# A recurrence in chunks: transition, input and output matrices formed ahead of the chain

## The chip, the cores and the metric

The kernel runs on one core of a Trainium2 chip. The metric is the device time of one execution in microseconds. Three runs of the kernel before took 3712.27, 3714.47 and 3717.64 us; the median is 3714.47 us. A change of 0.2%, about 7 us, is near what such runs can tell apart.

## What is computed

A two-layer encoder trunk over 1024 tokens of width 1024, in fp32: layer 0 mixes tokens by attention, layer 1 by a recurrence of the RWKV-7 kind in both directions, and each layer has an MLP. The change is in the recurrence of layer 1. Each of 16 heads holds a 64 x 64 state in each direction:

```python
def rwkv7_scan(r, w, k, v, kk, a):
    def step(state, inp):
        r_t, w_t, k_t, v_t, kk_t, a_t = inp
        sa = jnp.einsum('bhvk,bhk->bhv', state, -kk_t)
        state = (state * w_t[:, :, None, :] + sa[..., None] * (kk_t * a_t)[:, :, None, :]
                 + v_t[..., None] * k_t[:, :, None, :])
        return state, jnp.einsum('bhvk,bhk->bhv', state, r_t)
```

Direction 1 runs over the tokens backwards. The outputs are group-normed, gated and summed over the directions after this.

## The kernel before

The whole recurrence is in `rwkv_scan`. Tokens are cut into chunks of 64. Within a chunk the recurrence is written in closed form: with the decays divided out, the coupling between the tokens of a chunk is a strictly triangular 64 x 64 matrix per head, its unit-triangular inverse is applied to the chunk's inputs, and the state is carried from chunk to chunk.

The work goes by groups. A group is two chunks (128 tokens) of four heads (two pairs of heads) in both directions, so it has four chains (pair x direction, two heads in each) of two chunks each. Four groups are a batch, two batches are all tokens of four heads, and there are 32 groups. For each group:

- `prep` loads the group's decays, keys and receptances, makes exponentials, forms `zr` and `bk`, and multiplies them into `af` (L1266), which holds the coupling matrices in 64 columns and the in-chunk output matrices in the next 64. It masks `af` on POOL (L1270), transposes `bk` into `bn` (L1278, L1280) and writes the couplings to memory (`nd`, L1284). It runs eight groups ahead, in nine slots of buffers.
- `invert`, once a batch, reads the four diagonal 32 x 32 blocks of all couplings back, inverts them on DVE by 30 steps of two operations (L1297, L1299), writes them out, and puts them into `af` by DMAs (L1315, L1317).
- `post` makes the centered values (L1338 into `sv`) and completes the inverse's off-diagonal block by two products of 32 x 32 tiles (L1352, L1363).
- `scan` is the chain. For each chunk and each of the four chains: `c` <- coupling x values + `zr` x state (L1388, L1392); a copy of it to `y`, one half on ACT, the other on DVE (L1394, L1395); `c` <- inverse x `y` (L1397); copies into the other half of `sv` (L1399, L1400); `c` <- `bn` x `sv` (L1403); the new state `h` by two operations on DVE with the decay `pc` and the decayed old state `hd` that ACT made (L1386, L1412); and the output from `sv` and the old state (L1418, L1423), copied to `ot` (L1426). The operands of two heads stand in one 128-row matrix with zeros in the other head's place, so each product has 128 rows, and two heads write the two column halves of the array.
- `finish` does the group norm (L1445 is its one product), the gate and the sum, and stores.

The functions that do the side work are generators. After each chain's step of `scan`, `side` moves each of three lists of them on by a step. The order in which instructions then stand in the queues is set by a scheduler at build time, which goes by priorities (the chain's is raised) and its own times; at run time every engine works its queue in that order, and SP issues all these DMAs from one queue.

## Time and profile before

| | |
|---|---|
| profiled execution | 3712.8 us |
| its span on the core | 3710.7 us |
| granted TensorE clock over the span | 0.904 |
| PE, DVE, ACT, POOL busy over the span | 3197.8, 2596.9, 1854.2, 1850.4 us |
| L1266, first and last start (preparation) | 1937.9, 2756.2 us |
| first L1388 (chain) and last L1426 | 2122.2, 2909.2 us |

The span is one execution on the core. An engine's busy time is the time in which at least one of its instructions runs; matmuls are pipelined, so a busy PE need not be PE at its peak. PEld is the loading of weights, which overlaps PE. The recurrence with its preparation lies between about 1940 and 2915 us; attention and the first MLP are ahead of it, the output projection and the second MLP behind. A row of a view that groups instructions has: line, engine, operation, output<-inputs, shapes, count | busy us, mean ns of one | idle time of the engine just before, and what ended it.

### The profile page before, as it was taken

Reading aid. Unit: us, or ns where it says so; the run is one execution under the profiler, and the core shown is the slowest. Engines: PE = TensorE matmul, PEld = TensorE weight load, DVE = VectorE, ACT = ScalarE, POOL = GpSimd, SP = SyncE. Lnnn points to the kernel's source line nnn. Section 1 sums busy time; section 2 is a strip of 40 time slices with the busy share of each in tenths; the row PEclk is TensorE's granted clock in tenths of the full one; section 3 lists DMA queues with packets and bytes.
Section 4 is the critical chain, followed back from the end, with each engine's and each line's share of the span. In section 5 each row is a group of like instructions: output and inputs, shape, how many; then the busy total and the mean of one; then the engine's idle time right before and its main releaser. Section 6 shows DMA issues by size and latency. Waiting matters only on the chain. (4 is left out here: it accounts for less than half of the span.)

```text
span 3710.7 us, 61321 instructions
## 1 busy us (share of the span) xinstructions
PE 3197.8 (86%) x22168; PEld 2599.8 (70%) x22168; DVE 2596.9 (70%) x4617; ACT 1854.2 (50%) x4244; POOL 1850.4 (50%) x1642
## 2 busy tenths in 40 slices
PE   7999989799998978878888687787787889999998
PEld 6788987688777755555566575666666667887776
DVE  3355564744599979986963678888886565449996
ACT  2366564455543345654533365556566445554333
POOL 1000001655598877754566434444331146558887
PEclk9999999899999989879987587788787899999999
DMA  6222224232322032248766444444443413223023
GB/s 199 71 78 88 70 74 153 92 118 103 108 91 114 12 127 74 82 143 230 230 209 189 112 111 112 111 122 120 119 109 114 137 65 148 106 80 142 28 87 114
DMA packets 425100, 425.70 MB, mean 115 GB/s; under 512 B 138667, under 2 KB 338475, under 8 KB 418652
## 3 DMA queue, kind: packets, MB, share of 16 engines
q1 hardware_dynamic: 423612, 417.58, 36.3%
q0 software_dynamic: 1184, 4.20, 0.4%
q8 instruction: 174, 2.85, 0.3%
q14 instruction: 130, 1.06, 0.1%
HBM read 290.83 MB, written 138.20 MB: 116 GB/s over the span
## 5 line engine op out<-in xcount | busy, mean ns | idle before, releaser
L101 PE MATMUL pm<-bhi,lo 128*128 128x512 f32 x840 | 333.1, 399 | 46.3 <-DVE lo L130 46.1
L130 DVE TENSOR_TENSOR lo<-x,hi 128x512 fp32r<-128x512 f32 x300 | 322.1, 1080 | 61.8 <-ACT hi L129 61.7
L129 ACT ACTIVATE hi<-x 128x512 fp32r<-128x512 f32 x300 | 189.6, 633 | 323.4 <-DVE x L127 126.5
L100 PE MATMUL pm<-blo,hi 128*128 128x512 f32 x840 | 331.8, 395 | 8.6 <-POOL blo L130 8.1
L99 PE MATMUL pm<-bhi,hi 128*128 128x512 f32 x840 | 320.5, 394 | 5.4 <-ACT bhi L129 5.0
L127 POOL TENSOR_TENSOR x<-w1r 128x512 f32<-128x512 f32 x160 | 214.0, 1341 | 202.1 <-DVE lo L130 178.1
L130 POOL TENSOR_TENSOR blo<-bx,bhi 128x512 fp32r<-128x512 f32 x138 | 222.3, 1612 | 26.6 <-ACT bhi L129 26.0
L1270 POOL TENSOR_TENSOR af<-af,amask 128x512 f32<-128x512 f32 x128 | 163.8, 1286 | 136.7 <-ACT af L1269 111.9
L101 PEld LDWEIGHTS pm<-bhi,lo 128*128 128x128 f32 x840 | 158.4, 189 | 99.1 <-DVE lo L130 67.6
L905 POOL TENSOR_TENSOR wl<-wr,wh 128x512 fp32r<-128x512 f32 (+2 forms) x144 | 188.8, 1322 | 77.1 <-ACT wh L904 57.1
L1266 PE MATMUL A<-zr,bk 128*128 128x128 f32 x1024 | 187.4, 346 | 44.3 <-DVE bk L1259 38.1
L127 POOL TENSOR_TENSOR bx<-w 128x512 f32<-128x512 f32 x140 | 215.5, 1541 | 9.5
L886 DVE SCALAR_TENSOR_TENSOR x<-u,mu,x 128x512 f32<-128x512 f32 x192 | 208.4, 1121 | 7.9 <-ACT x L884 5.7
L1266 PEld LDWEIGHTS A<-zr,bk 128*128 128x128 f32 x1024 | 166.5, 249 | 58.6 <-POOL bk L1260 21.0
L127 DVE TENSOR_TENSOR x<-h 128x512 f32<-128x512 f32 x140 | 195.5, 1408 | 5.3 <-ACT h L268 2.7
L100 PEld LDWEIGHTS pm<-blo,hi 128*128 128x128 f32 x840 | 159.0, 189 | 49.5 <-POOL blo L130 16.0
L99 PEld LDWEIGHTS pm<-bhi,hi 128*128 128x128 f32 x840 | 159.3, 190 | 38.9 <-ACT bhi L129 5.9
L99 PE MATMUL mm<-xmh,wh 128*128 128x512 f32 x384 | 168.5, 460 | 17.0 <-ACT xmh L890 6.5
L1418 PE MATMUL c<-af,sv 128*64 128x64 f32 x1024 | 97.5, 275 | 79.8 <-DVE h L1412 71.2
L100 PE MATMUL mm<-xml,wh 128*128 128x512 f32 x384 | 157.1, 412 | 7.6 <-DVE xml L891 7.6
L1412 DVE SCALAR_TENSOR_TENSOR h<-c,pc,hd 64x64 f32<-64x64 f32 x448 | 126.8, 283 | 47.9 <-PE c L1403 30.3
L583 ACT ACTIVATE S<-S,mneg 128x256 f32<-128x256 f32 (+2 forms) x256 | 125.2, 501 | 67.0 <-DVE mneg L578 44.1
(370 smaller groups left out, 10044.3 us busy)
## 6 DMA issues: line engine op xcount, KB each, us to landing
w1r<-in_mlp_w_dram SPq DMA_DIRECT2D x32, 1024.0 KB, 5.4
w<-in_mlp_w_dram SPq DMA_DIRECT2D x32, 1024.0 KB, 5.5
x<-x SPq DMA_DIRECT2D x64, 386.0 KB, 3.4
hd<-h SPq DMA_DIRECT2D x24, 1024.0 KB, 4.2
h<-hd SPq DMA_DIRECT2D x24, 1024.0 KB, 7.8
wr<-in_w_rkv_dram SPq DMA_DIRECT2D x96, 256.0 KB, 2.8
rk<-rk SPq DMA_DIRECT2D x64, 256.0 KB, 3.9
x<-cs SPq DMA_DIRECT2D x32, 260.0 KB, 3.9
```

What stands on the lines that cost most here:

```text
L99: nc.tensor.matmul(out, lhsT=ahi, rhs=bhi, start=start, stop=False)
L100: nc.tensor.matmul(out, lhsT=ahi, rhs=blo, start=False, stop=False)
L101: nc.tensor.matmul(out, lhsT=alo, rhs=bhi, start=False, stop=stop)
L127: add.tensor_tensor(out=y, in0=x, in1=blocks[term[2]], op=ALU.add if term[1] == "+" else ALU.subtract)
L129: nc.scalar.activation(hi, x, AF.Copy)
L130: sub.tensor_tensor(out=lo, in0=x, in1=hi, op=ALU.subtract)
L583: nc.scalar.activation(s[:, :n], s[:, :n], AF.Exp, bias=mneg[:, i:i + 1], scale=-1.0)
L886: nc.vector.scalar_tensor_tensor(out=x, in0=at(2 * i), scalar=mu[:, i, c, kt:kt + 1], in1=x, op0=ALU.mult, op1=ALU.add)
L905: nc.gpsimd.tensor_tensor(out=wlo, in0=wr, in1=whi, op=ALU.subtract)
L1266: nc.tensor.matmul(ps[:, fsl(u, P)], lhsT=bk[:, u, j].rearrange("p a b -> p (a b)"), rhs=zr[:, u].rearrange("p a b -> p (a b)"), start=Tru ...
L1270: nc.gpsimd.tensor_tensor(out=o, in0=o, in1=consts["amask"].unsqueeze(1).to_broadcast([P, 4, P]), op=ALU.mult)
L1412: nc.vector.scalar_tensor_tensor(out=hn[rows, cols], in0=ch[rows, 128:192], scalar=pc[rows, u:u + 1], in1=hd[rows, cols], op0=ALU.mult, op ...
```

## The change

Everything that does not need the state is taken out of the chain. With the coupling's inverse, `post_a` and `post_b` now form for each chunk and head the matrix `w` = inverse x `zr` (first half of L1398), `u` = inverse x coupled values (L1374, L1398), and from them (L1409) the chunk's transition matrix (identity plus product, L1413) and its output matrix (L1415), both written over `zr`. `post_b` starts the sums of the new state (`h0`, `h1`, one bank for each chunk) and of the output (`o`) in PSUM. The chain then is: add transition x state to the bank that already holds the input's part, for the eight heads and directions (eight products of L1384), and one DVE operation over all four chains that multiplies by the decay (L1445). The output's part of the state is added to `o` beside it.

The layouts change with it. The operands of the two heads are no longer padded with zeros: in `prep`, products have 64 rows and the two heads use the two row halves of the array (L1265); elsewhere tiles are 64 x 64, the two chunks or the two heads on different halves of rows and of columns. `bk` is made by two operations for both heads. `bk` and `zr` are transposed as 128 x 128 (L1276, L1283). The couplings of one head and direction are written and read by DMAs of their own, four of L1287 for two before in a group, 32 of L1320 for 16 before in a batch. PSUM: two banks of A, two of B, one each of h0 and h1, two of o. The order of the side work is a written table over eight steps of a group in place of the three lists.

```diff
-        psC = pool("s_pc", 1, space=PSUM)
         psA = pool("s_pa", 2, space=PSUM)
-        psB = pool("s_pb", 1, space=PSUM)
+        psB = pool("s_pb", 2, space=PSUM)
+        psC = pool("s_pc", 2, space=PSUM)
...
+                bk = te.tile([P, 2, 4, RC], F32, tag="bk", name="bk", bufs=1)
+                nc.vector.tensor_tensor(out=bk[:, :, 1:3], in0=quad(kd), in1=quad(ipr), op=ALU.mult)
+                nc.gpsimd.tensor_tensor(out=bk[:, :, 0:4:3], in0=quad(a), in1=quad(ipr), op=ALU.mult)
...
+                        nc.tensor.matmul(ps[j][:, fsl(u, P)], lhsT=bku[rows, u], rhs=zr[rows, u // 2, :, u % 2, :],
+                                         start=True, stop=True)
...
+                    nc.tensor.transpose(ps[:, fsl(u, P)], bku[:, u], g.ident)
+                nc.scalar.activation(w.af[:, d].rearrange("p u j x -> p (u j) x")[:, :, P:AFX], c64(ps), AF.Copy)
...
+                        nc.tensor.transpose(ps[:, fsl(n, P)], w.zrd[:, n, 0].rearrange("p c t -> p (c t)"), g.ident)
+                    nc.scalar.activation(w.zrd[:, :, 0], ps.rearrange("p (n c t) -> p n c t", c=2, t=RC), AF.Copy)
...
-        def post(q, i):
+        def post_a(q, i):
...
+            ps = psb()
+            for un, n, j in UNITS:
+                for c in range(2):
+                    nc.tensor.matmul(ps[fsl(c, 64), fsl(un, RC)], lhsT=afd[fsl(1 - c, 64), 2 * n + c, j, 0:64],
+                                     rhs=w.sv[fsl(1 - c, 64), un, c, :], start=True, stop=True)
+            w.y = lp.tile([P, 8, RC], F32, tag="y", name="y")
+            nc.scalar.activation(w.y, c64(ps), AF.Copy)
+            yield
+
+        def sums(first, terms, end):
+
+            for k, (j, out, lhsT, rhs) in enumerate(terms):
+                with (tc.issue_after(first[j]) if first[j] is not None else ExitStack()):
+                    x = nc.tensor.matmul(out, lhsT=lhsT, rhs=rhs, start=first[j] is None, stop=end and k >= len(terms) - 2)
+                if first[j] is None:
+                    first[j] = x.ins
+
+        def post_b(q, i):
...
+            pw, pu = psb(), psb()
+            for ps, rhs in ((pw, lambda un: zrd[:, un // 2, 0, un % 2]), (pu, lambda un: w.y[:, un])):
+                for un, n, j in UNITS:
+                    for c in range(2):
+                        rows = fsl(c, 64)
+                        nc.tensor.matmul(ps[rows, fsl(un, RC)], lhsT=afd[rows, 2 * n + c, j, 0:64], rhs=rhs(un)[rows],
+                                         start=True, stop=True)
+            wt = lp.tile([P, 8, RC], F32, tag="wt", name="wt")
+            nc.scalar.activation(wt, c64(pw), AF.Copy)
+            for c in range(2):
+                nc.scalar.activation(sv[fsl(c, 64), :, c, :], c64(pu[fsl(c, 64)]), AF.Copy)
+            yield
+            pm = [psb(), psb()]
+            for un, n, j in UNITS:
+                for c in range(2):
+                    rows = fsl(c, 64)
+                    nc.tensor.matmul(pm[c][fsl(j, 64), fsl(n, P)], lhsT=wt[rows, un], rhs=afd[rows, 2 * n + c, j, 64:AFX],
+                                     start=True, stop=True)
+            for c in range(2):
+                pv = pm[c].rearrange("p (n t) -> p n t", t=P)
+                nc.vector.tensor_tensor(out=zrd[:, :, 0, c, :], in0=pv[:, :, 64:P],
+                                        in1=eye2.unsqueeze(1).to_broadcast([P, 4, 64]), op=ALU.add)
+                nc.vector.tensor_tensor(out=zrd[:, :, 1, c, :], in0=pv[:, :, 0:64], in1=zrd[:, :, 1, c, :], op=ALU.add)
+            yield
...
+            for c in range(2):
+                if not (w.last and c == 1):
+                    sums(w.fh[c], [(j, w.hb[c][fsl(j, 64), fsl(n, RC)], afd[:, 2 * n + c, j, P:AFX], sv[:, un, c, :])
+                                   for un, n, j in UNITS], first and c == 0)
+            for c in range(2):
+                sums(w.fo, [(j, w.ob[fsl(j, 64), fsl(2 * n + c, RC)], sv[:, un, c, :], afd[:, 2 * n + c, j, 64:P])
+                             for un, n, j in UNITS], False)
...
+                h = hs[0]
+                with tc.high_priority(50):
+                    if not (w.last and c == 1):
+                        if h is not None:
+                            sums(w.fh[c], [(j, w.hb[c][fsl(j, 64), fsl(n, RC)], zrd[fsl(j, 64), n, 0, c, :],
+                                               h[fsl(j, 64), n, :]) for un, n, j in UNITS], True)
+                        hs[0] = hp.tile([P, 4, RC], F32, tag="h", name="h")
+                        nc.vector.tensor_tensor(out=hs[0], in0=c64(w.hb[c][:, 0:256]),
+                                                in1=w.pc.rearrange("p d u -> p (d u)")[:, c::2].unsqueeze(2).to_broadcast([P, 4, RC]),
+                                                op=ALU.mult)
+                if h is not None:
+                    sums(w.fo, [(j, w.ob[fsl(j, 64), fsl(2 * n + c, RC)], h[fsl(j, 64), n, :],
+                                       zrd[fsl(j, 64), n, 1, c, :]) for un, n, j in UNITS], c == 1)
...
-                                nc.scalar.activation(hd, h, AF.Copy, scale=pc[:, u:u + 1])
...
-                            nc.scalar.activation(y[0:64, 1], ch[0:64, 0:64], AF.Copy)
-                            nc.vector.tensor_copy(y[64:128, 0], ch[64:128, 0:64])
...
+            s, p = scan(q, i, hs), of(prep, G + NQ - 1)
+            pa, pb = of(post_a, G + 2), of(post_b, G + 1)
+            run(s, 1)
+            for k in range(8):
+                if k == 1 or k == 3:
+                    run(s, 1)
+                if k in (0, 2, 5):
+                    run(pb, 1)
+                run(p, 1)
+                if k in (1, 3, 4, 6):
+                    run(pa, 1)
+                if i == 0 or (i == 1 and k < 7) or i > 1:
+                    run(gi, 1)
+                if k == 7:
+                    run(gi, 1)
+                    run(gi, 1)
+                if k in (2, 5):
+                    run(fin, 1)
```

How the queues look. First PE, in a group in the middle of the recurrence, before. Each `c_` number is one chain's bank for one chunk; a row is an instruction as the program has it, with the shape of its output.

```order
L1397 MATMUL c_22431<-y_17542,af 64x64 x2
L1278 MATMUL A<-ident,bk 128x64 x4
L1388 MATMUL c_22497<-sv,af 64x64 x2
L1392 MATMUL c_22497<-h_17533,zr_19560 64x64 x2
L1418 MATMUL c_22332<-af,sv 64x64 x2
L1423 MATMUL c_22332<-zr_19209,h_17539 64x64 x2
L1388 MATMUL c_22460<-sv,af 64x64 x2
L1392 MATMUL c_22460<-h_17538,zr_19209 64x64
```

The chains' products stand in twos, each two of another chain, with a few products of the preparation between. Now PE after, about one half of a group; `h_22738` and `h_22739` are the banks of the two chunks' states.

```order
L1354 MATMUL B<-xt,af 32x32 x16
L1265 MATMUL A<-zr,bk 128x128 x8
L1384 MATMUL h_22738<-sv,af 64x64 x3
L1384 MATMUL h_22739<-sv,af 64x64 x4
L1365 MATMUL B<-af,qs 32x32 x16
L1384 MATMUL h_22739<-sv,af 64x64 x4
L1384 MATMUL o<-af,sv 64x64 x16
L1276 MATMUL A<-ident,bk 128x128 x4
L1384 MATMUL h_22738<-h,zr 64x64 x8
L1283 MATMUL A<-ident,zr 128x128 x4
L1374 MATMUL B<-sv,af 64x64 x16
```

The products come in runs of eight and sixteen, and of the chain itself stands here the one run of eight from `h` and `zr`; the second chunk's follows behind L1374. Last SP's queue where a batch's inverted blocks go into `af`, after; before, the same place has eight of `af` and two of `xt`, then the loads of the next group, then the other eight and two.

```order
L1320 DMA af<-xd 32x4x32 x6
L1322 DMA xt<-xd 32x16x32
L1320 DMA af<-xd 32x4x32 x8
L1322 DMA xt<-xd 32x16x32
L1320 DMA af<-xd 32x4x32 x8
L1322 DMA xt<-xd 32x16x32
L1320 DMA af<-xd 32x4x32 x8
L1322 DMA xt<-xd 32x16x32
L1467 DMA gt<-g_1_12507 128x2x128
L1468 DMA y<-y_12503 128x2x128
```

The blocks of a batch now stand in one run, each DMA of half the size, and the loads of gates, sums, preparation and values of the next group behind them.

More of the change, by code (lines that the diff above doesn't have):

```diff
@@ L1504, in rwkv_scan, with of, run @@
-        b1.drain()
-        NB = KT
-        hs = None
-        for G in range(4 * NB):
+        NB = KT
+        NG = 4 * NB
+        bs = {}
+        def of(f, G):
+            b = G // 4
+            if G >= NG:
+                return iter(())
+            if b not in bs:
+                bs[b] = Batch(b)
+            return f(bs[b], G % 4)
+        def run(x, n=None):
+            while n is None or n > 0:
+                if next(x, x) is x:
+                    return
+                n = n and n - 1
@@ L1508, in rwkv_scan @@
+        for G in range(4):
+            run(of(prep, G))
+        gi = invert(bs[0])
+        run(gi, 17)
+        run(gi, 1)
+        run(of(post_a, 0))
+        run(gi)
+        for G in range(4, NQ - 1):
+            run(of(prep, G))
+        run(of(post_b, 0))
+        run(of(post_a, 1))
+        hs = [None]
+        fin = iter(())
+        for G in range(NG):
             b, i = G // 4, G % 4
             q = bs[b]
-            if i == 0 and b % 2 == 0:
-                hs = [None] * 4
-            g2 = G + NQ - 1
@@ L1548, in rwkv @@
+            for x in (s, pb, p, pa, fin):
+                run(x)
+            if i == 1:
+                run(gi)
+            fin = finish(q, i)
+        run(fin)
 def rwkv(tc, g, ap, es_u, ru, h_in, layer_out):
```

280 lines of the change are left out of this document (90 added, 190 removed).

## The prediction

> **What bounds it now.** I began with the busy time of each engine by stage, then counted the groups in the recurrence, then read what TensorE waits for there, and last the prices of single operations. The first three rows below are one view (stretch in us, length, then busy us of PE, PEld, DVE, ACT and POOL with instruction counts, granted clock, DMA share, GB/s): the steady part of the recurrence, its last part in which nothing is prepared any more, and for comparison a stretch of the attention layer. The last two rows are the same view for the line L1445 alone.
>
> ```profile
> 2150.00:2764.00 614.00, 487.85 (x7713) 400.75 (x7713) 499.82 (x1318) 364.10 (x1207) 262.88 (x324) 0.81 0.46 118
> 2764.00:2915.00 151.00, 116.19 (x2076) 91.44 (x2074) 102.50 (x344) 91.03 (x318) 19.15 (x27) 0.77 0.43 122
> 600.00:700.00 100.00, 88.28 (x419) 71.99 (x417) 56.27 (x68) 45.11 (x92) 28.68 (x42) 0.93 0.24 85
> ...
> 2149.00:2763.00 614.00, 37.51 (x46) 9.60 (x46) 0.81 0.46 117
> 2763.00:2915.00 152.00, 12.46 (x18) 3.37 (x18) 0.78 0.43 122
> ```
>
> L1445 runs once per group as two instructions, so 23 groups pass in 614 us, 26.7 us each; the nine in the last part make eight steps of 151/8 = 18.9 us. No engine is full: per group PE is busy 488/23 = 21.2 us (at 0.81 of the clock), DVE 21.7, ACT 15.8, POOL 11.4. PE is idle 26.7 - 21.2 = 5.5 us a group. What it waits for (PE's waits from 2220 to 2720 us; total us, times, longest):
>
> ```profile
> PE c L1418 <- DVE h L1412: 60.3, 45, 4.3
> PE c L1397 <- DVE y L1395: 22.6, 22, 2.6
> PE c L1403 <- ACT sv L1400: 10.3, 13, 2.0
> PE c L1418 <- DVE h L1409: 2.5, 2, 1.3
> PE A L1266 <- DVE zr L1254: 2.5, 5, 0.8
> ```
>
> The first four, 95.7 us in 500, are 5.1 us per group, and all are links of the chain y, sv, h. So the recurrence is bound by the chain's round trips standing in PE's queue in program order, with PE and DVE each at four fifths behind it. In the last part, without preparation, PE is idle 35 of 151 us: the chain again.
>
> **The change on PE.** Prices of PE's instructions: rows of the timeline (start, us, line, shapes, count), at full clock unless said, then three lines with the time of one alone (min/median/max).
>
> ```profile
> 2471.39 2.05 PE L1266 MATMUL A<-zr,bk 128*128 128x128 f32 x16
> 2456.53 2.08 PE L1266 MATMUL A<-zr,bk 128*128 128x128 f32 x8
> 2467.89 0.64 PE L1338 MATMUL B<-center,v 128*64 128x64 f32 x16
> 2558.94 0.69 PE L1352 MATMUL B<-xt,af 32*32 32x32 f32 x30
> 2581.72 0.47 PE L1278 MATMUL A<-ident,bk 64*128 64x64 f32 x8
> 2555.74 1.12 PE L1445 MATMUL L<-osq,ones 128*128 128x512 f32 x2
> ...
> L1266 PE MATMUL A<-zr,bk x1024: 272/275/582, 1938.0 to 2756.2; 128*128 128x128 f32 x171
> L1397 PE MATMUL c<-y,af x1024: 221/222/370, 2124.0 to 2907.9; 128*64 128x64 f32 x171
> L1352 PE MATMUL B<-xt,af x1024: 191/191/258, 2117.3 to 2867.1; 32*32 32x32 f32 x171
> ```
>
> A product is two instructions here (L1266 stands 512 times in the program's 32 groups and 1024 times in the row), a transpose one. Taking the last one's own time off and dividing by the rest: 128 columns on the whole array (2.05 - 0.27)/15 = 0.119 us an instruction (second row, at half clock: 0.26); 64 columns on alternate halves of the array (0.64 - 0.22)/15 = 0.028; 32x32 tiles (0.69 - 0.19)/29 = 0.017; a transpose of 64 columns 0.05; L1445 1.1 the two. Alternate halves overlap: 0.028 is half of the 0.06 that 64 columns cost alone by the first row.
>
> Counted per group, before: L1266 32 x 0.119 = 3.8; L1278 16 x 0.05 = 0.8; 112 products of 64 columns (16 of L1338, 96 of the chain), 224 x 0.028 = 6.3; 32x32 64 x 0.017 = 1.1; L1445 1.1: together 13.1 us. After: L1265 has 16 products on half the rows in pairs, 32 x 0.06 = 1.9; L1409, new, the same 1.9; L1342 8 products of 128 columns on half the columns 1.0; 12 transposes of 128 columns 12 x 0.119 = 1.4; products of 64 columns again 112 (L1374 16, L1398 32, the additions to h0, h1 and o 64) 6.3; 1.1 and 1.1: 14.7 us. So PE gains no time from less work; it gets **1.6 us more** per group. The step that is not seen before is a pair of products on different row halves writing one bank (L1374, L1398, the scan's part of L1384; L1265 writes two banks). The nearest row is L1352, whose neighbours use different rows and different columns of one bank: alone an instruction of 32 columns would cost a quarter of 0.119, 0.030, and it takes 0.017, so they overlap. I take the overlap. Its other end, no overlap, adds 1.9 (L1265) + 1.9 (L1409) + 160 x 0.028 = 4.5, 8.3 us per group.
>
> The Trainium skill (TensorEngine Tiling (Array Packing), Gotcha 1: PSUM Pressure) says that different row tiles cannot access the same PSUM bank at the same time, which speaks against this change. By that rule the 8.3 us would fall due (but for L1265's 1.9, whose pairs write two banks); L1352's 0.017 does not agree with it for tiles in different columns, so I keep it as a rival.
>
> PE's busy time at full clock before is 21.2 x 0.81 = 17.2 us, 4.1 over the counted 13.1: turns between array shapes and waits too short to show. By the order of the two programs the shape changes 19.9 times a group before and 19.3 after; I keep the 4.1. After: 14.7 + 4.1 = 18.8 us at full clock. The clock follows how densely PE works: 0.81 here at 79% busy, 0.93 in the attention row at 88%. I take 0.93: 20.2 us.
>
> **The other engines.** DVE's rows, from the same 500 us but for L335, which is from 700 to 1300 us (names, shapes, count | busy us, mean ns | idle before):
>
> ```profile
> L1412 DVE SCALAR_TENSOR_TENSOR h<-c,pc,hd 64x64 f32<-64x64 f32 x260 | 73.6, 283 | 26.6 <-PE c L1403 18.9 <-ACT y L1394 0.9 <-ACT ot L1426 0.5
> L1395 DVE COPY y<-c 64x64 f32<-64x64 f32 x146 | 32.1, 225 | 5.9 <-ACT y L1394 3.2
> L1399 DVE COPY sv<-c 64x64 f32<-64x64 f32 x145 | 31.6, 226 | 23.3 <-PE c L1397 20.7
> L1259 DVE TENSOR_TENSOR bk<-x,ipr 64x256 f32<-64x256 f32 x72 | 55.7, 773 | 3.8 <-PE A L1278 2.4
> L1299 DVE TENSOR_TENSOR nb<-nb,xtmp 128x150 f32<-128x150 f32 x9 | 8.1, 898 | 0.2
> ...
> L335 DVE TENSOR_TENSOR acc<-acc,pm 128x512 f32<-128x512 f32 x120 | 74.0, 674 | 0.0
> ```
>
> Removed per group: 16 h at 0.283 = 4.5, 8 y and 8 sv at 0.226 = 3.6, two of four bk = 1.5. Added: two h and four zr operations of 256 elements a partition, with one input from PSUM. Not seen; between 0.283 (64 elements, L1412) and 0.674 (512, L335), by length 0.45: 2.7 us (1.7 to 4.0). DVE: 21.7 - 9.6 + 2.7 = 14.8 us. But the 60 steps of the inversion (L1299 and its partner; what is left of DVE's busy time after the other lines of this view is 5.9 us a group, 23.6 a batch of four) stand in two groups of each four, so these have 14.8 + 5.9 = 20.7 us and the others 8.9. That is just below PE's 21.5: DVE is **the next bound**.
>
> ```profile
> L1386 ACT ACTIVATE hd<-h,pc 128x128 f32<-128x128 f32 x130 | 52.3, 402 | 62.7 <-DVE h L1412 57.2 <-DVE h L1409 4.1
> L1269 ACT ACTIVATE af<-A 128x512 f32<-128x512 f32 x72 | 41.2, 594 | 28.1 <-PE A L1266 14.4 <-PE c L1423 7.0 <-PE c L1418 6.5
> L1426 ACT ACTIVATE ot<-c 128x64 f32<-128x64 f32 x146 | 31.2, 220 | 13.5 <-PE c L1423 11.8 <-PE c L1418 0.3 <-PE c L1388 0.2
> L1280 ACT ACTIVATE bn<-A 128x256 f32<-128x256 f32 x72 | 26.4, 376 | 6.9 <-PE A L1278 6.6
> ...
> L1260 POOL TENSOR_TENSOR bk<-x,ipr 64x256 f32<-64x256 f32 x72 | 58.0, 805 | 16.3 <-ACT af L1269 5.3 <-ACT sv L1400 4.8 <-PE A L1278 3.5
> L1342 POOL MEMSET sv<- 64x512 f32 x36 | 18.7, 519 | 25.8 <-PE c L1423 16.1 <-PE c L1403 4.1 <-ACT ot L1426 3.4
> ...
> L1315 SPq DMA_DIRECT2D af<-xd x128: 303/450/1816, 2110.7 to 2840.5; - x128
> L1284 SPq DMA_DIRECT2D nd<-af x64: 577/610/635, 1995.0 to 2760.6; - x64
> ```
>
> ACT loses 8 each of hd 0.402, ot 0.220, and y and sv at about the same 0.22, and four bn at 0.376: 10.0 us. It gets seven copies of 512 elements a partition at 0.594 (two af, zr, y, wt, two sv) and two of 256 at 0.376: 4.9. So 15.8 - 5.1 = 10.7. POOL loses two bk (0.805) and two clearings (0.519): 11.4 - 2.6 = 8.8. Neither bounds; but each copy is now a wait of PE's queue, so their latency counts where PE has nothing ahead. SP issues per group two more nd and four more af: at most 2 x 0.61 + 4 x 0.45 = 3.0 us. In the new order the 32 af and 4 xt of a batch stand in one run, 36 x 0.45 = 16.2 us, and gt, y, x and v for the next group are queued behind it, and behind these ACT's first operation of a preparation and PE's L1265. In a group of 21.5 us this can cost a few us once in four; I give 0.75 us a group for it.
>
> **Waits left, and the sum.** The chain is now eight products and one DVE operation, twice a group: 2 x (16 x 0.028 + 0.22 + 0.45) = 2.2 us of a group, and other products stand between its links in PE's order. The waits on y, sv and h go (5.1 us). What stays is 0.5 us of other waits, and I add 0.75 for SP: idle 1.3. Group: 20.2 + 1.3 = **21.5 us** against 26.7. In the last eight steps PE's counted work before is 6.3 + 1.1 + 1.1 = 8.5; after, with as many products of 64 columns, it is 8.5 + 1.9 (L1409) + 1.0 (L1342) = 11.4; overhead 14.5 x 0.77 - 8.5 = 2.7, and 0.8 more for shapes (5.6 changes a group before, 14.1 after; a tenth of a us each, half of 4.1/19.9). So 14.9/0.93 + 0.9 = 16.9 against 18.9. Saved: 23 x 5.2 + 8 x 2.0 = 136 us. Ahead of the first group the change puts one more post_a and a post_b, up to 4.5 + 1.9 + 1.0 + 1.1 = 8.5 us on PE, and takes 2.6 us of POOL out of each of eight preparations, up to 21; both lie in part beside the inversion, and I take zero. The profiled execution took 3712.8 us, 1.7 under the median 3714.47: 3712.8 - 136 + 1.7 = **3578 us**.
>
> **Rivals.**
>
> - *PE runs dense* (13%): clock 1.0, idle 0.5. Group 19.3, last steps 14.9 + 0.5 = 15.4: 23 x 7.4 + 8 x 3.5 = 198, 3516 us. For it: the chain's waits are nearly all of the idle time. Against: DVE's 20.7 in two of four groups.
> - *The chain goes, other waits come* (16%): half of the 5.5 us returns as waits on copies of ACT, DVE and SP, and the clock reaches 0.87 only. 18.8/0.87 + 2.75 = 24.4; last steps 14.9/0.85 + 2.2 = 19.7: 23 x 2.3 - 8 x 0.8 = 47, about 3667 us.
> - *All waits return* (12%), on the other side: PE's queue is in order, and each group has some twenty places at which it waits for a copy or another engine. If they cost 5.5 us as the chain did, the clock stays 0.81, and the 1.6 us more work shows: 18.8/0.81 + 5.5 = 28.7; last steps 14.9/0.77 + 4.4 = 23.8. 23 x 2.0 + 8 x 4.9 = 85 slower, 3800 us. It decides from 26.7 - 23.2 = 3.5 us of waits at that clock. Against: most of the waits have a burst of other products ahead of them.
> - *Small tiles don't overlap* (7%): (18.8 + 8.3)/0.93 + 1.3 = 30.4; last steps (14.9 + 6.4)/0.93 + 0.9 = 23.8: 124 slower, 3840 us. It decides from 4.8 of the 8.3 us, where the group is back at 26.7. Against: L1352's 0.017.
>
> **Numbers.** The forecast has 52%; its own range is 3520 to 3640. Changes under 0.2% (7 us) can't be told from none here. Faster: 0.52 + 0.13 + 0.15 of the second rival = 0.80. Slower: 0.12 + 0.07 less 0.01 = 0.18; same: 0.02. The range, 3470 to 3715, takes in the dense case and the second rival and leaves out the two slow ones (0.19).
>
> **What would show it.** Right: groups of 20 to 23 us by the finishing line L1474; PE's waits on h under 0.5 us a group; PE busy above 88% at a clock above 0.9; L1374 and L1398 starting 0.03 us apart at full clock. Wrong: the last at 0.06 (no overlap), L1409 or L1354 waiting for DVE's zr in the groups of the inversion (DVE is the bound), L1265 or L1342 waiting for DMAs (SP's run of 36), or a clock at 0.8 with waits spread over many lines (the second and third rival).

## The result and the profile after

The changed kernel takes 3775.86 us, the median of four runs (3771.37 to 3785.31), against 3714.28 before: a ratio of 1.0176, with a 95% interval of 1.0161 to 1.0191. It is 62 us slower, where 136 us less were forecast, and the time lies outside the range.

The profiled execution took 3777.8 us, with a span of 3776.0. The recurrence in the view by stretches (columns as in the prediction): the part with preparation and the last eight steps of the kernel after.

```profile
2170.00:2820.00 650.00, 489.47 (x8560) 412.65 (x8559) 267.37 (x659) 301.41 (x599) 210.63 (x231) 0.77 0.42 108
2820.00:2963.00 143.00, 110.24 (x2144) 90.62 (x2142) 59.12 (x141) 61.51 (x112) 12.37 (x15) 0.77 0.43 119
```

The line of the finishing product, which runs as two instructions for each of the 32 groups, from the view of one line: count, duration min/median/max in ns, first and last start.

```profile
L1474 PE MATMUL A<-osq,ones x64: 592/595/1222, 2169.9 to 2964.1; 128*128 128x512 f32 x64
```

The same line of the kernel before:

```profile
L1445 PE MATMUL L<-osq,ones x64: 590/749/1223, 2149.8 to 2914.8; 128*128 128x512 f32 x64
```

The first group is finished 20 us later, 23 groups take 650 us in place of 614, and the last eight steps 143 in place of 151. From the last finishing product to the end of the span it is 3776.0 - 2964.1 = 811.9 us, and was 3710.7 - 2914.8 = 795.9. So 20 + 36 - 8 + 16 = 64 us, which is the difference of the spans but for rounding.

A group takes 650/23 = 28.3 us. PE is busy 21.3 of them, at 0.77 of its clock, and idle 7.0. DVE's busy time has fallen from 500 to 267 us and is nobody's bound as a sum. What PE waits for (the same 23 groups; total us, times, longest):

```profile
PE B L1342 <- ACT wt L1401: 47.5, 3, 16.6
PE B L1365 <- ACT qs L1358: 26.2, 8, 12.2
PE B L1354 <- issue: 24.8, 5, 7.8
PE B L1409 <- ACT sv L1345: 16.0, 3, 5.4
PE B L1354 <- DVE zr L1415: 13.1, 2, 7.2
...
PE h L1384 <- DVE h L1445: 8.5, 5, 3.3
```

The chain is nearly gone from this list: the wait on its state h, the last row, costs 8.5 us. What came in its place is fewer and longer waits, for copies of ACT and for DVE's zr, up to 16.6 us each. One of them, followed back, in the timeline of the kernel after (start, us, engine, line, count; in brackets the idle time before and who ended it):

```profile
2416.81 4.15 SPq L1320 DMA_DIRECT2D af<-xd  x6
...
2421.48 4.81 SPq L1320 DMA_DIRECT2D af<-xd  x8
...
2426.81 3.81 SPq L1320 DMA_DIRECT2D af<-xd  x8
...
2431.14 3.81 SPq L1320 DMA_DIRECT2D af<-xd  x8
...
2438.16 0.53 SPq L1239 DMA_DIRECT2D x<-x  x1
...
2441.57 0.42 ACT L1246 ACTIVATE ipr<-x 128x256 f32<-128x256 f32 x1 [15.88 <-DMA x<-x]
...
2442.98 0.78 ACT L1358 ACTIVATE qs<-B 32x256 f32<-32x256 f32 x2
...
2443.41 0.31 PE L1365 MATMUL B<-af,qs 32*32 32x32 f32 x2 [11.41 <-ACT qs L1358]
```

Read it from below. PE stands 11.4 us for the copy qs. ACT could have made that copy long before, but in its queue ipr stands ahead, and ipr waits 15.9 us for x. The load of x waits for nothing but its turn: SP issues it at 2438.16, behind the run of small DMAs of af and xt that began at 2416.81 and four loads of gt and y. This group took 40 us. One of the three waits of L1342 for wt, 16.3 us long and ended at 2318.55, is of the same kind: ACT's wt stands behind an ipr that waits 18.7 us for x. Five of the 23 groups took 40 to 46 us, the others 12 to 32.

### The profile page after: what moved, and what is told of

It is laid out like the page before. It is cut to its first block, busy times and chain, and to the rows that moved or that the text cites. A ratio compares the mean times of both kernels' runs of the same rounds, so it can differ in the third digit from the quotient of the medians.

```text
span 3776.0 us, 62124 instructions
## 1 busy us (share of the span) xinstructions
PE 3194.5 (85%) x23512; PEld 2604.2 (69%) x23512; DVE 2289.9 (61%) x3749; ACT 1766.8 (47%) x3412; POOL 1776.5 (47%) x1501
## 4 chain that ended last, share of the span: by engine, by line
PE 19%; DVE 10%; issue 5%; DMA 5%; SPq 5%; POOL 4%; ACT 3%; POOLq 0%; ACTq 0%; DVEq 0%
PE pm L101 3%; PE pm L99 3%; PE pm L100 3%; SPq L1320 3%; DVE lo L130 2%; DVE acc L335 2%; POOL af L1270 1%; DVE xtmp L1301 1%; DVE nb L1303 1%; PE h L1384 1%; PE o L1384 1%; DMA nb<-nd 1%; PE mm L99 1%; PE mm L100 1%; PE mm L101 1%
## 5 line engine op out<-in xcount | busy, mean ns | idle before, releaser
L1265 PE MATMUL A<-zr,bk 64*128 64x128 f32 x1024 | 113.9, 358 | 70.5 <-POOL bk L1257 30.1
L335 DVE TENSOR_TENSOR acc<-acc,pm 128x512 f32<-128x512 f32 x256 | 158.2, 675 | 0.6 <-PE pm L101 0.6
L1265 PEld LDWEIGHTS A<-zr,bk 64*128 64x128 f32 x1024 | 94.0, 251 | 84.1 <-POOL bk L1257 38.1
L101 PE MATMUL mm<-xmh,wl 128*128 128x512 f32 x384 | 147.6, 414 | 3.4 <-POOL wl L905 3.4
```

What stands on the lines that cost most here:

```text
L101: nc.tensor.matmul(out, lhsT=alo, rhs=bhi, start=False, stop=stop)
L335: dve.tensor_tensor(out=a, in0=a, in1=banks[j], op=ALU.add if sign == "+" else ALU.subtract)
L1265: nc.tensor.matmul(ps[j][:, fsl(u, P)], lhsT=bku[rows, u], rhs=zr[rows, u // 2, :, u % 2, :], start=True, stop=True)
```

## The experiments

The names E1 to E16 are those used in the expectations; there is no E4. All times are medians, and ratios are to the kernel before, timed beside each group of experiments.

### E1: as many DMAs as before

The table af is laid out with the chunk outermost, so that one DMA takes what two took: 2 nd a group and 16 af a batch again, with the same bytes.

```diff
-            w.af = sp.tile([P, 2, 4, 2, AFX], F32, tag="af", name="af")
+            w.af = sp.tile([P, 2, 2, 2, 2, AFX], F32, tag="af", name="af")
...
-                            for j in range(2):
-                                nc.sync.dma_start(out=afd[fsl(2 * c + k, 32), c::2, j, fsl(k, 32)],
-                                                  in_=q.xd[k, c, fsl(i, 8)][j::2].transpose([1, 0, 2]))
+                            nc.sync.dma_start(out=afu[fsl(2 * c + k, 32), c, :, fsl(k, 32)],
+                                              in_=q.xd[k, c, fsl(i, 8)].transpose([1, 0, 2]))
```

> The changed kernel with af laid out by chunk outermost, so that one DMA moves both heads: two nd per group and 16 af per batch, as before the change, with the same bytes. Theory S (SP's queue: the run of 36 issues holds up the next group's loads, and ACT and PE wait for these): SP is rid of 16 x 0.49 + 8 x 0.66 = 13 us of issues a batch; the long group of each batch (40 to 46 us against 20 to 28 in the others) shortens by 8 to 13 us, 3776 falls to 3690 to 3725. Theory C (PE's queue waits for the new copies of ACT and DVE, whatever SP does): within 10 us of 3776.

3727.83 us, ratio 1.0035 (1.0015 to 1.0055): 48 of the 62 us are back, 3 us short of the range of theory S. Its executions spread more than those of the others, from 3714 to 3745. In its trace the 23 groups take 606 us in place of 650, and the longest of them 36.5 us in place of 46.3, so it is the long groups that got shorter. The number of small DMAs is most of the loss, and yet taking it away brings none of the gain that was forecast.

### E2: the DMAs of af from ACT's queue

```diff
-                                nc.sync.dma_start(out=afd[fsl(2 * c + k, 32), c::2, j, fsl(k, 32)],
+                                nc.scalar.dma_start(out=afd[fsl(2 * c + k, 32), c::2, j, fsl(k, 32)],
```

> The changed kernel with its 32 af DMAs of a batch issued from ACT's queue, nothing else. S: SP loses 16 us of issues a batch, the loads no longer stand behind them; ACT is busy 45% and pays the issues: 3690 to 3740. C: ACT, for whose copies PE waits, is held up by some 13 us a batch: 3790 to 3850.

3762.98 us, ratio 1.0124 (1.0106 to 1.0143), in neither range: 13 us better than with all DMAs on SP, where E1 got 48. The run of 32 issues now stands in another in-order queue, with ACT's copies behind it; in its 23 groups ACT's copy wt waited 26.3 us behind the DMAs of af. Splitting the load over two queues helps little where the second one also carries what PE waits for.

### E3: no DMAs of af

The inverted blocks are not put back into af, so this part of the computation is left out.

```diff
-                        for k in range(2):
-                            for j in range(2):
-                                nc.sync.dma_start(out=afd[fsl(2 * c + k, 32), c::2, j, fsl(k, 32)], ...
```

> The changed kernel without the DMAs that put the inverted 32x32 blocks back into af (32 a batch; af keeps the masked couplings there), all else kept. S: the long group goes, every group is 20 to 26 us, 3630 to 3680. C: 3760 or more, the waits on copies stay.

3695.17 us, ratio 0.9946 (0.9926 to 0.9966): a bound for that run, 81 us, and still only 21 us under the kernel before beside it (3716.38). The range expected of theory S was missed by 15 us.

### E5: the kernel before with its DMAs doubled

```diff
-                            nc.sync.dma_start(out=afv[fsl(2 - 2 * j + k, 32), :, j, fsl(k, 32)],
-                                              in_=q.xd[k, j, fsl(i, 8)].transpose([1, 0, 2]))
+                            for s in range(2):
+                                nc.sync.dma_start(out=afv[fsl(2 - 2 * j + k, 32), fsl(s, 4), j, fsl(k, 32)],
+                                                  in_=q.xd[k, j, fsl(2 * i + s, 4)].transpose([1, 0, 2]))
```

(and the same for nd)

> The kernel before with its nd and af DMAs cut in two, as many as in the changed kernel and of the same size. S: SP has 11.9 us of issues in a group of 26.7 and gets 3.3 more, which its slack can take in part: 3715 to 3745. If the doubled DMAs alone are the loss, whatever the chain: 3770. C: 3714, as the copies are not there.

3734.66 us, ratio 1.0053 (1.0038 to 1.0068), as theory S expected. Doubling the number of DMAs costs the kernel before 18 us and the changed one 48. So the price of a DMA in a queue depends on the kernel around it; that it is what stands behind it in the queue is read from the timeline above, not tested by this run.

### What E1 still waits for

After E1 the question was open why a kernel without the chain and with the old number of DMAs is not faster. Its 23 groups, of E1:

```profile
2161.00:2767.00 606.00, 487.13 (x8562) 407.34 (x8560) 268.59 (x660) 300.58 (x599) 209.01 (x231) 0.80 0.46 115
```

What PE and DVE wait for in 500 us of them, of E1:

```profile
PE B L1354 <- issue: 42.9, 5, 12.0
PE B L1409 <- ACT sv L1403: 23.3, 4, 8.7
...
DVE xtmp L1302 <- DMA nb<-nd: 38.3, 5, 10.3
```

PE is idle 606 - 487 = 119 us, nearly as long as in the kernel before (614 - 488 = 126). The second row is the chain of the kernel after again, shorter: in all five of these waits sv stands in ACT's queue behind an ipr that waits 6.0 to 9.6 us for x. The largest row says "issue", which means that the profile shows nothing that PE waited for. The timeline of E1 around one of these waits shows it:

```profile
2446.15 2.74 SPq L1296 DMA_DIRECT2D nb<-nd  x2
...
2452.99 0.20 DVE L1302 TENSOR_TENSOR xtmp<-nb 128x30 f32<-128x30 f32 x1 [6.59 <-DMA nb<-nd]
...
2459.30 0.38 DVE L1302 TENSOR_TENSOR xtmp<-nb 128x210 f32<-128x210 f32 x1
...
2460.00 0.42 DVE L1413 TENSOR_TENSOR zr<-B,eye 128x256 f32<-128x256 f32 x1
2460.34 0.41 DVE L1415 TENSOR_TENSOR zr<-B,zr 128x256 f32<-128x256 f32 x1
...
2460.85 1.07 PE L1354 MATMUL B<-xt,af 32*32 32x32 f32 x32 [6.85 <-issue]
2460.96 0.42 DVE L1257 TENSOR_TENSOR bk<-x,ipr 128x256 f32<-128x256 f32 x1
...
2461.46 0.42 ACT L1247 ACTIVATE ipr<-x 128x256 f32<-128x256 f32 x1 [9.20 <-DVE bk L1257]
```

DVE stands 6.6 us for the load of nb, then does 20 of the inversion's 60 steps (each operation of L1302 and L1304 counted as one), and only then zr. PE's next product needs a bank B; there are two, and zr is what frees one: PE starts 0.1 us after the second zr ends. bk stands behind the same steps, and ACT's ipr, with ACT's other copies behind it, waits 9.2 us for bk. In E1's trace 17 to 22 steps stand together ahead of a zr in both groups of an inversion; before, with 32 small operations of the chain in each group, nearly all steps stood among them in runs of one to four (215 of 218 runs, the longest eight). This gave theory D, that the place of the inversion in DVE's queue is what holds the kernel, against theory P, that the handovers of the preparation between ACT, POOL and DVE through single buffers do. A third thing in E1's timeline, two shapes of product in turn, is priced in E9 below.

### E6 and E7: the steps of the inversion behind the main work

E6 is E1 with each step placed behind the latest zr, bk or h of the program ahead of it. E7 also loads nb at the end of the group before and spreads the steps evenly over the two groups. In the cut below the first two lines are E6's, the rest E7's.

```diff
+                with (tc.issue_after(late[0]) if late[0] is not None else ExitStack()):
                     nc.vector.tensor_tensor(out=tv, in0=nb[:, 0:t, t:t + 1].to_broadcast([P, t, n]), ...
...
-                if i == 0 or (i == 1 and k < 7) or i > 1:
+                if i < 2:
                     run(gi, 1)
-                if k == 7:
-                    run(gi, 1)
-                    run(gi, 1)
...
+            if i == 3:
+                gi = invert(bs[b + 2]) if b + 2 < NB else iter(())
+                run(gi, 1)
```

> The merged kernel (E1, 3727.8 us), and in DVE's queue each step of the inversion is placed behind the latest operation of the main work that stands ahead of it in the program, so that runs of up to 20 steps no longer stand ahead of a zr in the first group of an inversion (2 do). Theory D (what holds PE in E1's 118 us of idle time over 23 groups is DVE's queue: zr and bk stand behind the inversion's steps and behind the step that waits for nb): the 42.9 us of waits at the 32x32 products shrink, those at the products wt by a half of 49.3; 3690 to 3720. But the first two steps still wait for nb ahead of zr, so not all goes. Theory P (single buffers of ipr and bk and the copies of the preparation set the pace whatever DVE's order is): 3720 to 3745.

> As the run before (steps behind the main work), and nb is loaded one eighth of a group earlier, at the end of the group before, with the 60 steps spread evenly over the two groups (no triple portion at the end of the first). Theory D: the wait for nb at the head of DVE's queue (38 us in 500 in E1) goes too, PE's idle time over the 23 groups falls from 118 to below 60 us, and the granted clock rises from 0.80 to 0.85 or more: 3640 to 3690. Theory P: 3715 to 3745, idle time as in E1.

E6: 3690.86 us, ratio 0.9937 (0.9922 to 0.9952). E7: 3685.76, ratio 0.9911 (0.9891 to 0.9930). The same instructions in another order on one engine give 37 and 42 us, within what theory D expected, and both are faster than the kernel before. But E7's idle time fell only from 119 to 596 - 498 = 98 us, not below 60, and the clock rose only to 0.81: right in time, wrong in how. The 23 groups of E7:

```profile
2150.00:2746.00 596.00, 497.87 (x8554) 415.19 (x8552) 292.41 (x670) 301.01 (x600) 208.82 (x232) 0.81 0.47 120
```

The gain isn't where theory D put it either. E6's trace is 24 us shorter than E1's, but 17 of them lie ahead of the first finishing product (2144.6 in place of 2161.1) and 7 in the last steps; the 23 groups give 5, and 4 are lost behind. In E7's trace the groups give 10 of 26. The runs of steps were moved, not dissolved: 20 to 22 still stand ahead of a zr in an inversion's second group (in E7 another 12 in its first), and DVE still waits 35 (E6) and 30 us (E7) for nb. What went within the groups is ACT's wait for x: their traces show none. So these two runs show that the order matters, and mostly ahead of the groups, where the first inversion stands; what the steps cost within the groups is shown by E8.

### E8: E1 without the 60 steps

The inversion's steps are left out; the identity stands in place of the inverse, and loads and stores stay.

```diff
-                nc.vector.tensor_tensor(out=tv, in0=nb[:, 0:t, t:t + 1].to_broadcast([P, t, n]), ...
-                nc.vector.tensor_tensor(out=nb[:, 0:t, t + 1:32], in0=nb[:, 0:t, t + 1:32], in1=tv, op=ALU.add)
+            nc.gpsimd.memset(nb, 0.0)
```

> The merged kernel with the 60 DVE steps of the inversion left out (work left out: the inverse is replaced by the identity, one clearing on POOL; loads and stores of the blocks stay). Theory D: the waits at the 32x32 products and at the products wt fall by at least two thirds, idle time over the 23 groups below 50 us, clock 0.85 or more; 3600 to 3660. Theory P: DVE is emptier but the handovers of the preparation stay: 3700 to 3730.

3646.06 us, ratio 0.9815 (0.9795 to 0.9835): 82 us under E1; the traces differ by 66, and 49 of these lie in the 23 groups. Theory P alone is out. PE's idle time fell from 119 to 58 us in 23 groups, a little short of what D expected, but the clock stayed at 0.82, as its row of the 23 groups shows:

```profile
2143.00:2699.00 556.00, 497.53 (x8550) 411.17 (x8550) 154.66 (x360) 299.31 (x598) 214.13 (x236) 0.82 0.49 125
```

Where the clock is lost, in stretches of 3.4 us of E8's trace:

```profile
2378.10:2381.50 3.40, 1.71 (x23) 1.34 (x22) 2.79 (x8) 2.29 (x6) 0.88 (x2) 1.00 0.71 199
2381.50:2384.90 3.40, 3.40 (x61) 2.99 (x62) 0.00 (x0) 1.79 (x4) 3.05 (x3) 0.50 0.29 82
2384.90:2388.30 3.40, 3.40 (x19) 2.46 (x18) 0.00 (x0) 0.00 (x0) 0.00 (x0) 0.50 0.42 119
2388.30:2391.70 3.40, 3.40 (x24) 2.70 (x24) 0.42 (x1) 0.00 (x0) 0.00 (x0) 0.50 0.49 113
2391.70:2395.10 3.40, 3.40 (x55) 3.07 (x55) 1.11 (x3) 2.08 (x5) 1.41 (x2) 0.50 1.06 148
```

and in its timeline (E8's L1361 and L1380 are the lines 1365 and 1384 of the kernel after):

```profile
2381.47 1.15 PE L1361 MATMUL B<-af,qs 32*32 32x32 f32 x32 [1.55 <-ACT qs L1354]
...
2384.43 0.47 PE L1380 MATMUL o<-af,sv 128*64 128x64 f32 x2
2384.83 0.47 PE L1380 MATMUL h<-h,zr 64*64 64x64 f32 x2
2385.24 0.47 PE L1380 MATMUL o<-af,sv 128*64 128x64 f32 x2
```

One wait of 1.55 us leaves PE busy for 1.71 of 3.4 us, and the next four stretches run at half clock, though the records show PE busy through all of them. In the middle two it issues only 19 and 24 instructions: two shapes of product alternate in pairs, 0.40 us a pair. Nearly all stretches of half clock in the traces here last 3.4 us or a multiple of it (64 of 65 in E8's). The Trainium skill (TensorE: Matmul & The Clock Gate, What's actually happening) has the same window of about 3.4 us, and says that one busy window brings the full clock back. Here three that the records show as busy did not.

The traces tell more if one counts work in place of busy time. Take for each stretch of 3.4 us the products that begin in it, and add up rows x columns of the tile x columns of the output / (128 x 128). In the five stretches above this is about 1090, 942, 400, 1024 and 1312, and only the last is followed by full clock. Over the 1356 stretches of the groups in eight traces (before, after, E1, E8, E9, E10, E14, E16), "1300 or more, then full clock next" is right in 91%; the best rule by busy share (60% or more) is right in 80%. By this count a group has 12% less work after the change than before (11200 against 12770), as the operands are no longer padded with zeros. It is a count, not an experiment: no run changed this work alone.

### E9: the alternating shapes in one block

E1, with the scan's h<-h,zr (64 rows) placed behind the last o<-af,sv (128 rows) of their group. In E1 there are 144 such turns in the 23 groups, 27.0 us from start to next start, summed over the trace.

```diff
-                            sums(w.fh[c], [(j, w.hb[c][fsl(j, 64), fsl(n, RC)], zrd[fsl(j, 64), n, 0, c, :], ...
+                            with tc.issue_after(w.fol):
+                                sums(w.fh[c], [(j, w.hb[c][fsl(j, 64), fsl(n, RC)], zrd[fsl(j, 64), n, 0, c, :], ...
```

> The merged kernel with the scan's products h<-h,zr placed behind the last product o<-af,sv of their group, so that the two shapes no longer alternate in pairs on PE (144 turns, 27.0 us of the 23 groups in E1). If PE's busy time sets the pace, 20 us go: 3700 to 3715. If the waits set it, less than 8 us: 3718 to 3735; the chain, whose start is later by up to a us a group, should cost nothing.

3691.58 us, ratio 0.9940 (0.9925 to 0.9954): 36 us, more than either expectation. The 23 groups of E9:

```profile
2162.00:2746.00 584.00, 436.74 (x8558) 372.07 (x8554) 268.67 (x660) 298.62 (x599) 209.24 (x232) 0.82 0.47 120
```

and one such block in its timeline:

```profile
2424.86 0.68 PE L1384 MATMUL h<-h,zr 64*64 64x64 f32 x16
```

The sixteen instructions take 0.68 us together, and PE is busy 437 us of the 23 groups in place of 487. But much of that comes back as waiting: idle time rises from 119 to 147 us. The 23 groups get 22 us shorter and the last steps 8 (136 to 128). The profiled execution of E1, 3714 us, was one of its fastest, so the medians lie further apart than the traces do.

### E10 to E12: the edits together, and the stages of post_a further apart

E10 is E7 and E9 together, with two buffers each for gt and y of the finishing. E11 is E9, and E12 is E10, with the stages of post_a spread (and h<-h,zr also behind the products that read qs, so that these two don't alternate):

```diff
-            gt = t2.tile([P, 2, 2, P], F32, tag="gt", name="gt", bufs=1)
-            y = t2.tile([P, 2, 2, P], F32, tag="y", name="y", bufs=1)
+            gt = t2.tile([P, 2, 2, P], F32, tag="gt", name="gt")
+            y = t2.tile([P, 2, 2, P], F32, tag="y", name="y")
```

```diff
-                if k in (1, 3, 4, 6):
+                if k in (1, 3, 5, 7):
                     run(pa, 1)
```

> All three together on the merged kernel: the steps of the inversion behind the main work and nb loaded earlier (E7, 3685.8), the scan's h<-h,zr products behind the last o<-af,sv (E9, 3691.6), and gt and y of the finishing with two buffers each, so that the last groups' finishing doesn't wait for the one before. If the parts are independent: 3727.8 - 42 - 36 - about 8 for the end = 3642; 3630 to 3665. If they remove the same waits: 3675 to 3690.

> E9 (merged, no alternating shapes, 3691.6) and the stages of post_a an eighth of a group further apart, so that other products stand between the 32x32 products that make qs and those that read ACT's copy of it. In E1 the waits there are 11 us in 23 groups, 1.3 to 1.9 each. Theory W (a wait costs what it lasts): 3680 to 3690. Theory K (a window of 3.4 us in which PE works less than some two thirds is followed by 10 to 14 us at half clock, so that such a wait costs a group about 5 us in place of 1.5): 3625 to 3665, with a granted clock of 0.85 or more over the 23 groups.

> E10 with the stages of post_a further apart as in E11. Theory K: 3590 to 3630, groups of 22 us at a clock of 0.88 or more, near what was predicted of the change. Theory W: 10 us under E10.

E10: 3641.53 us, ratio 0.9796 (0.9771 to 0.9820). The parts add up: 48 for the DMAs, 42 for the steps, 36 for the turns and 8 for the end were expected to give 3642. That they do so to the microsecond is luck, as E1's executions alone spread over 31 us.

E11: 3700.28 us, ratio 0.9961 (0.9946 to 0.9976), 9 us over E9, and E12: 3652.55, ratio 0.9834 (0.9816 to 0.9852), 11 over E10. Both runs miss both theories, and theory K falls in the form in which it was put: the waits for qs did go in E11 (0.2 us left in 23 groups), but other waits came, idle time rose from 147 to 160 us, and the clock stayed at 0.82. That a short wait can be followed by half clock is seen in E8; that removing one such wait brings the clock back is not so here, where other waits came in its place.

### E13: all edits of E12, with the small DMAs

The changed kernel with its own layout of af, 4 nd a group and 32 af a batch, and every other edit of E12.

> The changed kernel with its small DMAs as they are (4 nd a group, 32 af a batch; nothing merged), and all the other edits of E12. If SP's run of 36 issues costs by itself (theory S): 40 to 60 us over E12, PE waiting for v and x in the long groups. If it only hurt together with DVE's queue: within 15 us of E12.

3720.22 us, ratio 1.0016 (1.0002 to 1.0030), 68 us over E12, timed beside it, and more than theory S expected. So the doubled DMAs do not only hurt together with DVE's queue; they cost no less once the rest is faster.

### E14, E15 and E16: what is left

E14 is E10 without the 60 steps, as in E8 (this work left out). E15 is E10 with two buffers for ipr. E16 keeps all steps, but leaves the first two eighths of each of the two groups free of them.

```diff
-                ipr = te.tile([P, 4, RC], F32, tag="ipr", name="ipr", bufs=1)
+                ipr = te.tile([P, 4, RC], F32, tag="ipr", name="ipr")
```

```diff
-                if i < 2:
+                if i < 2 and k > 1:
                     run(gi, 1)
```

> E10 (3641.5) with the 60 DVE steps of the inversion left out, as in E8 (work left out: the identity in place of the inverse, one clearing on POOL). In E10 TensorE still waits 44 us in 23 groups at the 32x32 products, now shown as waiting for DVE's zr. Theory D (what is left is DVE's share in the inversion's groups): idle time over the 23 groups from 106 to below 45 us, 3570 to 3605, the predicted 3578 within it. Theory P (the handovers of the preparation between ACT, POOL and DVE, and the half clock after each): 3615 to 3640.

> E10 with two buffers for ipr, so that ACT no longer waits for DVE's and POOL's bk (61 and 43 us in 450 in E10) with copies for PE queued behind it. Theory P: 15 to 35 us under E10. Theory D: within 8 us of E10, since bk itself stays late behind the steps.

> E10 (3641.5) with the inversion's steps left out of the first two eighths of its two groups, so that 1 and 14 of them, not 12 and 21, and no wait for nb stand ahead of a first zr in DVE's queue; all 60 steps are kept, and the blocks come back to af some 4 us later. Theory D (what is left is where the 60 steps stand in DVE's queue): 3605 to 3630, TensorE's waits at the 32x32 products from 44 to below 25 us in 23 groups. If it is DVE's amount of work that holds the groups, not its order: 3635 to 3650, the same waits at another place (the blocks af come late for the next batch, or the second zr behind 12 steps).

E14: 3562.21 us, ratio 0.9585 (0.9566 to 0.9604). E15: 3778.46, ratio 1.0170 (1.0153 to 1.0187). E16: 3630.39, ratio 0.9766 (0.9745 to 0.9788), the fastest version that does all the work. The waits of PE in the 23 groups of E10:

```profile
PE B L1357 <- DVE zr L1419: 25.9, 5, 6.1
...
PE A L1268 <- POOL bk L1260: 13.2, 3, 6.5
...
PE h L1387 <- DVE h L1451: 7.9, 4, 6.0
```

and of E16:

```profile
PE h L1387 <- DVE h L1451: 26.7, 11, 9.1
PE A L1268 <- POOL bk L1260: 26.2, 10, 5.4
PE B L1357 <- DVE zr L1419: 13.2, 5, 3.2
```

E16 halves the wait for zr, as theory D says, and gets 11 us, just outside the range and not clear of the spread (E10's executions go from 3632 to 3643, E16's from 3626 to 3636). More of the steps now stand ahead of h (53 in place of 36 in the traces' 23 groups), and the waits for h and bk grow. With the steps gone altogether E14 is 8 us below the range of theory D, and the groups take nearly what was forecast, in this row of E14:

```profile
2137.00:2639.00 502.00, 426.75 (x8560) 364.22 (x8562) 153.36 (x360) 299.12 (x599) 214.40 (x237) 0.86 0.54 139
```

502/23 = 21.8 us, against 21.5 forecast. That is luck: it comes from less work, at a clock of 0.86 in place of 0.93, with 75 us of idle time, more than D expected. So of the 79 us between E10 and E14 about 11 went with the steps' place, as far as E16 moved it; the rest has gone only where the steps were left out. Whether a better place would bring more of it wasn't tried.

E15 is 137 us over E10, a miss for both theories, and the plainest lesson. The wait that it takes away is replaced by a longer one, in E15's 23 groups (first ACT, then PE):

```profile
ACT ipr L1249 <- DMA x<-x: 226.4, 40, 13.0
...
PE B L1368 <- ACT qs L1361: 54.0, 25, 9.0
PE B L1413 <- ACT sv L1407: 46.3, 15, 9.5
```

With a second buffer the program's order puts ipr earlier into ACT's queue, ahead of copies that PE needs, and there it waits 226 us for x, whose loads come no earlier. The single buffer had kept it out of the way.

## Why the prediction was wrong, point by point

**The chain's waits go.** Right. Of PE's waits for links of the chain, those on h are left, 8.5 us in 23 groups, 0.4 a group.

**Prices of single operations.** Right. Of the kernel after, the view of groups for the 23 groups:

```profile
L1415 DVE TENSOR_TENSOR zr<-B,zr 128x256 f32<-128x256 f32 x46 | 19.1, 415 | 0.0
L1445 DVE TENSOR_TENSOR h<-h,pc 128x256 f32<-128x256 f32 x43 | 18.1, 421 | 74.3 <-PE h L1384 72.2 <-PE B L1398 2.0
L1401 ACT ACTIVATE wt<-B 128x512 f32<-128x512 f32 x23 | 13.7, 595 | 20.5 <-PE B L1398 20.5
```

0.42 us against the 0.45 taken for DVE's new operations, and 0.595 against 0.594 for ACT's copies. The sums of whole engines were less exact: DVE 267/23 = 11.6 us a group where 14.8 were forecast, ACT 301/23 = 13.1 for 10.7, POOL 9.2 for 8.8.

**Products on row halves of one bank overlap.** Right, for halves that also differ in columns, and the rival that they don't is out. Two rows of the kernel after's timeline:

```profile
2479.63 1.15 PE L1398 MATMUL B<-y,af 64*64 64x64 f32 x32
...
2483.29 1.09 PE L1409 MATMUL B<-af,wt 64*64 64x128 f32 x16
```

The first row gives (1.15 - 0.22)/31 = 0.030 us an instruction, not 0.06. The second, with 128 columns and two banks, gives (1.09 - 0.27)/15 = 0.055, near the 0.06 that was taken. In the program the pairs of L1374, L1398 and L1384's scan lie on different halves of rows and of columns, as L1352's tiles did; a pair on the same columns of one bank doesn't occur, so that case stays open. The Trainium skill's rule (TensorEngine Tiling (Array Packing), Gotcha 1: PSUM Pressure), by which the 0.06 would fall due, does not agree with L1398's 0.030. The prediction exempted only L1265 from that rule; L1409's pairs write two banks as well (`pm[c]`), so its 1.9 us would not have fallen due by it either.

**PE's work: too high.** 489.47 x 0.77/23 = 16.4 us a group at full clock, where 18.8 were forecast. The overhead of 4.1 us that was kept was too much. A part of what is left can be avoided: the turns, as E9 shows. This error of 2.4 us hid part of the two that follow.

**The clock of 0.93: failed.** It was read from the share of time in which PE is busy, with a row of another layer beside it. It fell to 0.77, and stayed at 0.82 in E8, where PE is busy 498 of 556 us, the share of that row. So the busy share does not set the clock. The work done on the array in each stretch tells it better (the count at E8), but what lowers it is not settled by a run. Even E14 has 0.86. In this term alone a group lost 16.4/0.77 - 16.4/0.93 = 3.7 us.

**Idle time of 1.3 us: failed, in two steps.** It came to 7.0. With the two terms above, 5.7 + 3.7 - 2.4/0.93 = 6.8 us, which is the whole of 28.3 - 21.5.

The first is the line "In a group of 21.5 us this can cost a few us once in four; I give 0.75 us a group for it". The run of DMAs was seen, and so was what stands behind it, but it was priced as a delay of a few us in a queue with slack. It is worth 48 us (E1) to 68 us (E13 against E12), 2 to 3 us a group, and the timeline shows the way: everything behind it is in order too, x, then ipr on ACT, then the copies, then PE. The sign that was named for it, a wait of L1342 or L1265 for DMAs, shows in the profile as a wait for ACT, one link further on.

The second is DVE's 20.7 us in two groups of each four, called just below PE's bound. As a sum it was too high: E8 without the steps has 155/23 = 6.7 us a group, so the steps are 4.9 a group and 9.8 in each of the two, some 16.5 together. But the sum was the wrong question. That the chain's 32 operations had held the inversion's steps apart in DVE's queue was not seen. Without them up to 25 steps, and the wait for nb, stand ahead of zr and bk. With the steps out 79 to 82 us go, 49 (E8) and 61 (E14) of them in the traces' 23 groups. By order alone 37 to 42 us go, of which the traces put 5 and 10 in the 23 groups. The wait was named in the list of what would show the prediction wrong (L1354 waiting for DVE's zr), but no price stood beside it and no chance.

**Lead-in taken as zero: off by 20 us, and 16 us behind the recurrence were not thought of.** The first group's finish came at 2169.9 in place of 2149.8. With fewer DMAs it came at 2161.1 (E1), with the steps behind the main work as well at 2144.6 (E6), so these two are what it was lost to. At the end the last groups follow so closely that the finishing's single buffers gt and y, still in use by the group before, hold its loads back in E1's timeline; with two buffers, and the other edits, E10 needs 3641.3 - 2835.8 = 805.5 us behind the last finishing product, and has 6 of the 16 back. Where the other 10 went was not followed.

**The rivals.** The one that all waits return had 12% and came nearest: 28.7 us a group at a clock of 0.81 against 28.3 at 0.77. Its mechanism, many waits for copies as long as the chain's together, was not what happened: most of the loss is a few long ones. Its last steps of 23.8 us were wrong; they took 17.9, between the 18.9 before and the 16.9 of the forecast; there nothing is prepared any more.

## What to carry to other kernels

A chain that sets the pace also spaces out what stands in the other in-order queues; before taking it away, list for each queue what will then stand in a row, and price the longest run by who stands behind it, link by link up to the engine that matters, rather than by its share of a group. Then look in the trace for where a gain came, not only whether it came. Here 62 us slower became 84 us faster with the same arithmetic, by fewer DMAs, by another place of 60 small operations and by not alternating array shapes. A single buffer can be what keeps an operation out of a queue where it would block others: look at what a freed operation waits for next.

## What was not expected of the hardware

These DMAs hold SP's queue for about as long with half the bytes. Rows of the kernel after, whose DMAs of nd and af carry half the bytes of those before (0.610 and 0.450 us there):

```profile
L1320 SPq DMA_DIRECT2D af<-xd x256: 303/430/1730, 2084.8 to 2887.8; - x128
...
L1287 SPq DMA_DIRECT2D nd<-af x128: 574/608/1790, 1999.5 to 2817.4; - x128
```

And TensorE can be shown as busy for three stretches of 3.4 us on end without the full clock coming back (E8's rows). The number of instructions doesn't tell a stretch that brings it back: 61 in the first did not, 55 in the fourth did. The work on the array, rows x columns x output columns, tells it in 91% of the stretches counted, with the line near 1300 of it in 3.4 us; by this measure small tiles add little. No run varied it alone.
